# A hybrid encoder on one core: memory tokens turned by strips from row tile 4 on, one tile at a time, and later loads of natural tokens

## The chip, the core and the metric

The kernel runs on one core of one Trainium2 chip. The core has TensorE (PE: matmuls, with weight loads shown as PEld), VectorE (DVE), ScalarE (ACT), GpSimd (POOL) and SyncE (SP), and 16 DMA engines that move data between the chip's main memory and the core's on-chip memory. Engines run their own instructions in order and wait for each other by semaphores. The metric is the device time of one execution in microseconds; a kernel's time is the median of its runs.

## What is computed

Two layers of an encoder over 256 tokens of width 2048, all in float32. Each layer projects the normalised tokens, mixes them in three head groups, projects back and adds. The third group attends to 256 memory tokens, whose keys and values come from a projection that does not depend on x:

```python
for l in range(DEPTH):                                    # DEPTH = 2
    proj = rmsnorm(x, norm_g[l]) @ w_in[l]                # 2048 -> 7168, split in ten parts
    y_a = short_gated_conv(...) * silu(a_g)               # 768 columns
    y_d = rmsnorm(diff_attention(...), ...) * silu(d_g)   # 768 columns
    mkv = rmsnorm(mem, mem_norm_g[l]) @ w_mem_kv[l]       # mem: 256 x 2048 -> 512 keys, 512 values
    y_m = memory_attention(mq, mk, mv) * silu(m_g)        # 512 columns
    x = x + concat(y_a, y_d, y_m) @ w_out[l]
```

## The kernel before, in words

**Matrix products.** Every float32 operand is split into a high part (written by ACT) and a low part (the rest, written by DVE), and a product is three matmuls: high by high, high by low, low by high. Stationary operands are tokens with the contracted columns on the partitions, so tokens must be turned; moving operands are weights, 512 columns at a time. `split_T` (L257) writes both parts of one turned row tile (128 columns of all 256 tokens) into `memT` or `xT`.

**The memory stage** comes first: keys and values of both layers, before any work on x. It is one hand-written loop over 32 chunks g, sixteen row tiles k for each of two layers (L893 to L955). Chunk g multiplies row tile k of the memory tokens by 128 rows of `w_mem_kv[l]`, 1024 columns: half 0 is keys, half 1 values, two tiles of tokens, three matmuls each, so twelve matmuls. `operands(g)` (L812) prepares a chunk two chunks ahead: `token_parts` turns and splits the tokens (first layer alone), `w_parts` (L787) scales the weights by the norm's gain and splits them. `beside(g)` (L856) issues what stands beside the chunk: weights of chunk g + 4 (four raw buffers), loads and squares listed in the dictionaries `TOKENS`, `MEM_STRIPS`, `X_STRIPS`, `X_NATURAL`, `X_SQUARES`, and one small load of constants per chunk. `pin` keeps the program's order on an engine; what is not pinned is placed by the planner.

**Two ways of turning tokens.** Row tiles below `DEALT` (8) are loaded as natural tokens into `xs`, and TensorE turns them with an identity (`turned`, L795, two transposes per tile, into `pt`). Row tiles from `DEALT` on are loaded by strips: `strips_of` (L676) loads 512 columns of all tokens in four transfers of 128 KB, each to 32 partitions; DVE then turns blocks of 32 x 32 (`strips_turned`, L686), 128 x 1024 values in one instruction, which gives four row tiles at once. Their contracted columns are dealt over four tiles (column 4p + j to partition p of tile j), so the weights' rows are taken in the same order (`x_row_tiles`) and their gains from `gm_dealt` instead of `cva`. Natural tokens of all tiles are needed anyway for the sums of squares (`mem_squares`, ACT), from which `mem_stats` makes the row scales `stm`. x is turned by strips too (`x_turned`, L692), and its natural tokens are loaded into the same `xs` (`x_natural`) when the memory tokens there are done with; they are squared (`x_square`) and kept for the residual.

**Steps.** `run_side` (L231), at the end of each chunk, advances every generator in `tasks` that is due; `yield n` means n chunks until the next step. `later(g, n)` sets the first.

**The end of the stage.** When a layer's last row tile is done, `empty_keys` (L833) copies the key sums from PSUM (`kraw`, ACT) and `empty_values` (L839) the value sums, scaled by `stm`. Four accumulators exist; the first block of products over x (`block`, L293, called at L980) needs those that `kraw` frees. `keys_slowly` then normalises keys and turns them by transfers that POOL issues. `rest_of_constants` (L147) turns the small vectors into columns on TensorE.

**The rest** is twice: blocks over x in chunks of two row tiles (`load_w`, L280; ACT writes hi, DVE lo; PE L310 to L312), attention beside them, and the projection back.

Of the kernel before, what the change touches and what calls it, by code (L numbers as in the profile page):

```python
# [19 lines left out]
P = 128  # L20
D_MODEL = 2048
SEQ = 256
# [15 lines left out]
NA = P // B  # L38
PAIR_EVERY = 9
QT = NB // P  # L40
DEALT = 8


C_X, C_B, C_C, C_G = 0, 768, 1536, 2304
# [5 lines left out]
def encoder(ctx: ExitStack, tc: tile.TileContext, x, mem, norm_g, w_in, conv_w, conv_b,  # L50
# [21 lines left out]
    def nm(s):  # L72
        uid[0] += 1
        return f"{s}_{uid[0]}"
# [54 lines left out]
    def g_norm(l, k):  # L129
        return gx[:, l * KT + k:l * KT + k + 1]  # L130
# [83 lines left out]
    def later(g, n):  # L214
        due[id(g)] = chunk[0] + n
        return g
# [40 lines left out]
    def split_T(dst, k, src, gain, pin=False):  # L257

        hi, lo = dst[:, 0, k, :], dst[:, 1, k, :]
        if gain is None:  # L260
            both = (nc.scalar.copy(hi, src),
                    nc.vector.tensor_tensor(lo, src, hi.bitcast(F32), ALU.subtract))
        else:
            both = (nc.scalar.activation(hi, src, AF.Copy, scale=gain),
                    nc.vector.scalar_tensor_tensor(lo, src, gain, hi.bitcast(F32), ALU.mult, ALU.subtract))
        if pin:
            for i in both:
                tc.keep_in_program_order(i)
        made.add((id(dst), k))
# [403 lines left out]

    mem_done = set()

    def strips_of(src, at_once=1):  # L676

        st = tmp.tile([P, SEQ // B, B * QT], F32, tag="e", name=nm("xt"))
        for b in range(NA):
            pin(nc.sync.dma_start(  # L680
                st[b * B:(b + 1) * B], src[:, b * B * QT:(b + 1) * B * QT].rearrange("(n p) r -> p n r", p=B)))
            if (b + 1) % at_once == 0 and b + 1 < NA:
                yield
        return st

    def strips_turned(st):  # L686
        whole = tmp.tile([P, QT, SEQ], F32, tag="sh", name=nm("xf"))
        pin(nc.vector.transpose(whole.rearrange("p j (n i) -> p j n i", i=B),  # L688
                                st.rearrange("p n (c j) -> p j n c", j=QT)))
        return whole  # L690

    def x_turned(dst, l, q, src, at_once):  # L692


        st = yield from strips_of(src, at_once)
        yield 2
        whole = strips_turned(st)
        yield
        for j in range(QT):
            split_T(dst, q * QT + j, whole[:, j], g_norm(l, q * QT + j), pin=True)  # L700
            if j % 2:
                yield

    def x_next(dst, l, q):

# [25 lines left out]
    def mem_squares(c):  # L731

        for t in range(NT):
            sq = tmp.tile([P, NB], F32, tag="nat", name=nm("msq"), bufs=3)
            pin(nc.scalar.activation(sq, xs[:, t, c * NB:(c + 1) * NB], AF.Square, accum_out=ssm[:, t, c:c + 1]))
# [62 lines left out]
            pin(nc.tensor.transpose(pt[:, t * P:(t + 1) * P], xs[:, t, k * P:(k + 1) * P], ident))  # L798
        return pt

    dealt = {}

    def mem_turned(q, at_once):
        st = yield from strips_of(mem[:, q * NB:(q + 1) * NB], at_once)
        yield 2
        dealt[q] = strips_turned(st)

    def token_parts(g):
        if g < KT:
            split_T(memT, g, turned(g) if g < DEALT else dealt[g // QT][:, g % QT], None, pin=True)  # L810

    def operands(g):  # L812
        token_parts(g)
        w_parts(g)

    accs = {}

# [29 lines left out]
    def x_natural(c, t):  # L847
        pin(nc.sync.dma_start(xs[:, t, c * NB:(c + 1) * NB], x[t * P:(t + 1) * P, c * NB:(c + 1) * NB]))

    TOKENS = {0: 4, 1: 6, 8: 8, 9: 10, 10: 12, 11: 14}  # L850
    MEM_STRIPS = {2: 2, 4: 3}
    X_STRIPS = {12: 0, 16: 1, 20: 2, 24: 3}
    X_NATURAL = {14: (0, 0), 17: (0, 1), 20: (1, 0), 22: (1, 1), 24: (2, 0), 26: (2, 1), 28: (3, 0), 29: (3, 1)}
    X_SQUARES = {19: 0, 25: 1, 29: 2}

    def beside(g):  # L856


        if g + 4 < NG:
            if g in TOKENS:  # L860
                tokens(TOKENS[g], 2)
            weights(g + 4)
        if g in MEM_STRIPS:
            tasks.append(later(mem_turned(MEM_STRIPS[g], 2 if g == 2 else 1), 1))
        if g >= 2:
            for dst, src in islice(constants, 1):
                pin(nc.sync.dma_start(dst, src))
        if g in X_STRIPS:
            q = X_STRIPS[g]
            tasks.append(later(x_turned(xT, 0, q, x[:, q * NB:(q + 1) * NB], 1), 1))  # L870
        if g in (4, 8, 11, 13):
            mem_squares((4, 8, 11, 13).index(g))
        if g == 6:
            distance(1)
        if g == 13:
            tasks.append(later(mem_stats(), 1))
        if g == 21:
            tasks.append(later(rest_of_constants(), 1))
        if g in X_NATURAL:
            x_natural(*X_NATURAL[g])  # L880
        if g in X_SQUARES:
            for t in range(NT):
                x_square(X_SQUARES[g], t)

    row_sums = []

    def last_square():
        for t in range(NT):
            x_square(3, t)
        yield 2  # L890
        row_sums.append(stats_of(ssx, "st"))

    for _ in range(DEPTH):  # L893
# [7 lines left out]
    tokens(1, 1)  # L901
    weights(1, 0, NB)
    weights(1, NB, NB)
    tokens(2, 1)
    weights(2, 0, NB)
    weights(2, NB, NB)
    tokens(3, 1)
    weights(3)
    warm(6)
    distance(0)  # L910
    pv = ps_t.tile([P, NB], F32, tag="t", name="pva")
# [250 lines left out]
```

## Time and profile before

| | us |
|---|---|
| median of 3 runs (917.89 to 918.72) | 918.6 |
| the profiled execution | 918.26 |
| its span | 916.5 |
| PE busy in the span | 912.1 |
| DVE busy | 682.3 |
| ACT busy | 512.4 |
| first product of the memory stage | 5.04 |
| first product over x | 94.96 |

The granted TensorE clock is 1.000 over the span. Rows of the timeline read: start, duration (both us, from the span's start), engine, line, operation, output<-inputs, shape, count of merged instructions, and in brackets the idle time before it with what ended it. Rows of groups read: line, engine, operation, output<-inputs, shape, count | busy us, mean ns of one | idle us before them, and what ended it. Rows of windows read: stretch, its length, then busy us and count for PE, PEld, DVE, ACT and POOL, granted clock, DMA share, GB/s. SPq rows are issues of transfers by SP. 216 MB are moved in all, 236 GB/s over the span.

### The profile page before, as it was taken

Reading aid. Unit: us, or ns where it says so; the run is one execution under the profiler, and the core shown is the slowest. Engines: PE = TensorE matmul, PEld = TensorE weight load, DVE = VectorE, ACT = ScalarE, POOL = GpSimd, SP = SyncE. Lnnn points to the kernel's source line nnn. Section 1 sums busy time; section 2 is a strip of 40 time slices with the busy share of each in tenths; the row PEclk is TensorE's granted clock in tenths of the full one; section 3 lists DMA queues with packets and bytes.
Section 4 is the critical chain, followed back from the end, with each engine's and each line's share of the span. In section 5 each row is a group of like instructions: output and inputs, shape, how many; then the busy total and the mean of one; then the engine's idle time right before and its main releaser. Section 6 shows DMA issues by size and latency. Waiting matters only on the chain.

```text
span 916.5 us, 12329 instructions
## 1 busy us (share of the span) xinstructions
PE 912.1 (100%) x4167; PEld 758.0 (83%) x4167; DVE 682.3 (74%) x1216; ACT 512.4 (56%) x802; POOL 7.0 (1%) x18
## 2 busy tenths in 40 slices
PE   9999999999999999999999999999999999999998
PEld 7888888888888888888888888888888888888887
DVE  5888978857897787658677757878899786658553
ACT  6766745675554765545455544568555664446431
POOL 0001000000000000000000000000000000000000
PEclk9999999999999999999999999999999999999999
DMA  9999888876769989978687867886888979978662
GB/s 286 291 270 310 273 253 235 254 211 185 187 212 239 247 249 266 264 255 249 214 257 249 237 195 221 235 237 176 242 231 222 254 206 260 288 228 241 210 216 80
DMA packets 252964, 216.11 MB, mean 236 GB/s; under 512 B 131727, under 2 KB 180197, under 8 KB 252901
## 3 DMA queue, kind: packets, MB, share of 16 engines
q1 hardware_dynamic: 250740, 211.78, 80.5%
q0 software_dynamic: 672, 2.10, 0.6%
q10 hardware_dynamic: 1488, 1.46, 0.5%
q8 instruction: 32, 0.52, 0.2%
q14 instruction: 32, 0.25, 0.1%
HBM read 194.32 MB, written 20.97 MB: 235 GB/s over the span
## 4 chain that ended last, share of the span: by engine, by line
PE 91%; DMA 4%; DVE 2%; ACT 1%; issue 1%; SPq 0%; ACTq 0%; DVEq 0%
PE acc L311 29%; PE acc L310 29%; PE acc L312 29%; DMA raw<-in_w_mem_kv_dram 3%; PE po L480 1%; PE acc L827 1%; DMA raw<-in_w_in_dram 1%; DVE xf L688 1%; DVE lo L793 1%; ACT hi L792 1%; PE poT L469 1%; PE s L594 1%; PE s L593 1%; PE s L646 1%; DMA xt<-in_mem_dram 0%
## 5 line engine op out<-in xcount | busy, mean ns | idle before, releaser
L290 DVE TENSOR_TENSOR lo<-raw,hi 128x1024 fp32r<-128x1024 f32 x288 | 351.4, 1222 | 171.0 <-ACT hi L289 167.5
L289 ACT CAST hi<-raw 128x1024 fp32r<-128x1024 f32 x288 | 302.2, 1052 | 305.5 <-PE acc L312 235.9
L311 PE MATMUL acc<-lo,xT 128*128 128x512 f32 x896 | 349.2, 390 | 0.0
L312 PE MATMUL acc<-hi,xT 128*128 128x512 f32 x896 | 348.7, 389 | 0.0
L310 PE MATMUL acc<-hi,xT 128*128 128x512 f32 x896 | 347.7, 390 | 0.2 <-ACT kraw L836 0.2
L312 PEld LDWEIGHTS acc<-hi,xT 128*128 128x128 f32 x896 | 168.2, 188 | 34.7
L310 PEld LDWEIGHTS acc<-hi,xT 128*128 128x128 f32 x896 | 168.2, 188 | 34.7 <-ACT kraw L836 0.6
L311 PEld LDWEIGHTS acc<-lo,xT 128*128 128x128 f32 x896 | 168.3, 188 | 33.7
L312 PE MATMUL acc<-hi,yT 128*128 128x512 f32 (+1 forms) x258 | 100.0, 387 | 0.0
L310 PE MATMUL acc<-hi,yT 128*128 128x512 f32 (+1 forms) x258 | 100.0, 387 | 0.0
L311 PE MATMUL acc<-lo,yT 128*128 128x512 f32 (+1 forms) x258 | 99.9, 387 | 0.0
L827 PE MATMUL acc<-hi,memT 128*128 128x512 f32 (+1 forms) x260 | 70.5, 389 | 0.0
L310 PEld LDWEIGHTS acc<-hi,yT 128*128 128x128 f32 x258 | 48.4, 188 | 10.0
L311 PEld LDWEIGHTS acc<-lo,yT 128*128 128x128 f32 x258 | 48.4, 188 | 9.9
L312 PEld LDWEIGHTS acc<-hi,yT 128*128 128x128 f32 x258 | 48.4, 188 | 9.8
L827 PEld LDWEIGHTS acc<-hi,memT 128*128 128x128 f32 x260 | 47.9, 188 | 9.8 <-ACT hi L792 0.3
L827 PE MATMUL acc<-lo,memT 128*128 128x512 f32 (+1 forms) x130 | 39.7, 387 | 0.0
L827 PEld LDWEIGHTS acc<-lo,memT 128*128 128x128 f32 x130 | 24.3, 188 | 5.0
L793 DVE SCALAR_TENSOR_TENSOR lo<-raw,cva,hi 128x1024 fp32r<-128x1024 f32 (+2 forms) x21 | 21.4, 1026 | 6.5 <-ACT hi L792 5.4
L604 ACT ACTIVATE e<-e,mx 128x256 f32<-128x256 f32 x48 | 23.8, 498 | 1.4 <-DVE mx L600 1.3
L793 DVE SCALAR_TENSOR_TENSOR lo<-raw,gm_dealt,hi 128x1024 fp32r<-128x1024 f32 x16 | 20.5, 1279 | 4.6 <-ACT hi L792 4.5
L792 ACT ACTIVATE hi<-raw,cva 128x1024 fp32r<-128x1024 f32 (+2 forms) x21 | 19.7, 947 | 6.4 <-DMA raw<-in_w_mem_kv_dram 6.4
(162 smaller groups left out, 654.6 us busy)
## 6 DMA issues: line engine op xcount, KB each, us to landing
raw<-in_w_in_dram SPq DMA_DIRECT2D x192, 512.0 KB, 4.4
raw<-in_w_out_dram SPq DMA_DIRECT2D x64, 512.0 KB, 4.7
raw<-in_w_in_dram SPq DMA_DIRECT2D x64, 256.0 KB, 4.8
raw<-in_w_mem_kv_dram SPq DMA_DIRECT2D x29, 512.0 KB, 7.1
d<-sh SPq DMA_DIRECT2D x88, 128.0 KB, 3.9
sh<-d SPq DMA_DIRECT2D x72, 128.0 KB, 3.9
xt<-in_x_dram SPq DMA_DIRECT2D x16, 128.0 KB, 6.7
xs<-in_x_dram SPq DMA_DIRECT2D x8, 256.0 KB, 6.8
```

The costliest lines, as they stand in the source:

```text
L289: nc.scalar.copy(hi, raw)
L290: nc.vector.tensor_tensor(lo_, raw, hi.bitcast(F32), ALU.subtract)
L310: nc.tensor.matmul(acc[t], sh, hi, start=first, stop=False)
L311: nc.tensor.matmul(acc[t], sh, lo, start=False, stop=False)
L312: nc.tensor.matmul(acc[t], sl, hi, start=False, stop=last)
L469: nc.tensor.matmul(po, vp[:, v_part, k], e[:, e_part, k], start=k + v_part + e_part == 0, stop=k == NT - 1 and v_part == 1)
L480: nc.tensor.matmul(po[:, t, :], eT[:, i, t, k, :], v[:, k, h * P:(h + 1) * P], start=k == 0, stop=k == NT - 1)
L593: nc.tensor.matmul(s[c][:, i, :], qi, k_first(yT, c, h), start=True, stop=False)
L604: nc.scalar.activation(e[:, c, i], e[:, c, i], AF.Exp, bias=mx[:, c, i:i + 1], accum_out=sm[:, c, i:i + 1])
L792: pin(nc.scalar.activation(hi, raw, AF.Copy, scale=gain))
L793: pin(nc.vector.scalar_tensor_tensor(lo, raw, gain, hi.bitcast(F32), ALU.mult, ALU.subtract))
L827: pin(nc.tensor.matmul(accs[l, half][t][:, at:at + n], memT[:, token_part, k, t * P:(t + 1) * P], p, start=k == 0 and at == 0 and token_pa ...
```

## The change

- `DEALT` is 4: row tiles 4 to 7 of the memory tokens come by strips too, and are no longer turned on TensorE. This holds for weights and gains of both layers.
- Memory strips are turned one row tile at a time (`mem_turn`, 128 x 256 values), one tile ahead of its use, inside `operands`; x strips two row tiles at a time.
- Strips for tiles 4 to 7 are loaded ahead of the loop, with the first constant (`gm_dealt` of layer 0); tokens 2 and 3 come in one load. Weights of chunk 4 are split in two halves.
- Natural memory tokens 4 to 7 are loaded beside chunks 6 and 8 instead of 0 and 1; their squares, `mem_stats` and the other constants come later.
- Strips of x begin a chunk later, natural tokens of x two or more; those of the last 512 columns are loaded in the first block over x, where the last two pairs of squares are made.

```diff
-DEALT = 8
+DEALT = 4
...
-    def strips_turned(st):
-        whole = tmp.tile([P, QT, SEQ], F32, tag="sh", name=nm("xf"))
-        pin(nc.vector.transpose(whole.rearrange("p j (n i) -> p j n i", i=B),
-                                st.rearrange("p n (c j) -> p j n c", j=QT)))
-        return whole
+    def whole_tile():
+        return tmp.tile([P, QT, SEQ], F32, tag="sh", name=nm("xf"))
+
+    def turn_strips(whole, st, at, n):
+        pin(nc.vector.transpose(whole.rearrange("p j (n i) -> p j n i", i=B)[:, at:at + n],
+                                st.rearrange("p n (c j) -> p j n c", j=QT)[:, at:at + n]))
...
-        whole = strips_turned(st)
-        yield
-        for j in range(QT):
-            split_T(dst, q * QT + j, whole[:, j], g_norm(l, q * QT + j), pin=True)
-            if j % 2:
-                yield
+        whole = whole_tile()
+        for j in range(0, QT, 2):
+            turn_strips(whole, st, j, 2)
+            yield
+            for i in (j, j + 1):
+                split_T(dst, q * QT + i, whole[:, i], g_norm(l, q * QT + i), pin=True)
...
+    def mem_strips(q, at_once, apart=1):
+        strips_in[q] = yield from strips_of(mem[:, q * NB:(q + 1) * NB], at_once, apart)
+
+    def mem_turn(k):
+        q, j = divmod(k, QT)
+        if j == 0:
+            dealt[q] = whole_tile()
+        turn_strips(dealt[q], strips_in[q], j, 1)
...
     def operands(g):
+        if g == DEALT:
+            mem_turn(g)
         token_parts(g)
-        w_parts(g)
+        if DEALT <= g < KT - 1:
+            mem_turn(g + 1)
+        if g == DEALT:
+            w_parts(g, 0, NB)
+            w_parts(g, NB, NB)
+        else:
+            w_parts(g)
...
-    TOKENS = {0: 4, 1: 6, 8: 8, 9: 10, 10: 12, 11: 14}
-    MEM_STRIPS = {2: 2, 4: 3}
-    X_STRIPS = {12: 0, 16: 1, 20: 2, 24: 3}
-    X_NATURAL = {14: (0, 0), 17: (0, 1), 20: (1, 0), 22: (1, 1), 24: (2, 0), 26: (2, 1), 28: (3, 0), 29: (3, 1)}
-    X_SQUARES = {19: 0, 25: 1, 29: 2}
+    TOKENS = {6: 4, 8: 6, 9: 8, 10: 10, 11: 12, 12: 14}
+    MEM_SQUARES = {4: 0, 11: 1, 13: 2, 14: 3}
+    MEM_STRIPS = {2: 2, 5: 3}
+    X_STRIPS = {13: 0, 17: 1, 21: 2, 25: 3}
+    X_NATURAL = {16: (0, 0), 19: (0, 1), 22: (1, 0), 25: (1, 1), 28: (2, 0), 30: (2, 1)}
+    X_SQUARES = {23: 0, 27: 1}
...
-        if g >= 2:
+        if g >= 10:
             for dst, src in islice(constants, 1):
                 pin(nc.sync.dma_start(dst, src))
...
-        if g in (4, 8, 11, 13):
-            mem_squares((4, 8, 11, 13).index(g))
+        if g in MEM_SQUARES:
+            mem_squares(MEM_SQUARES[g])
...
-        if g == 13:
+        if g == 14:
             tasks.append(later(mem_stats(), 1))
-        if g == 21:
+        if g == 28:
             tasks.append(later(rest_of_constants(), 1))
...
-    def last_square():
+    def last_squares():
+        for t in range(NT):
+            x_natural(3, t)
+            yield
+        for t in range(NT):
+            x_square(2, t)
+        yield 2
         for t in range(NT):
             x_square(3, t)
-        yield 2
+        yield
         row_sums.append(stats_of(ssx, "st"))
...
-    tokens(2, 1)
+    tokens(2, 2)
     weights(2, 0, NB)
     weights(2, NB, NB)
-    tokens(3, 1)
     weights(3)
+    for _ in mem_strips(1, NA):
+        pass
+    for dst, src in islice(constants, 1):
+        pin(nc.sync.dma_start(dst, src))
...
-    tasks.append(later(last_square(), 2))
+    tasks.append(later(last_squares(), 1))
```

More of the change, by code (lines that the diff above doesn't have):

```diff
@@ L674, in encoder, with strips_of @@
     mem_done = set()
-    def strips_of(src, at_once=1):
+    def strips_of(src, at_once=1, apart=1):
         st = tmp.tile([P, SEQ // B, B * QT], F32, tag="e", name=nm("xt"))
@@ L682, in strips_of @@
             if (b + 1) % at_once == 0 and b + 1 < NA:
-                yield
+                yield apart
         return st
-    def strips_turned(st):
-        whole = tmp.tile([P, QT, SEQ], F32, tag="sh", name=nm("xf"))
-        pin(nc.vector.transpose(whole.rearrange("p j (n i) -> p j n i", i=B),
-                                st.rearrange("p n (c j) -> p j n c", j=QT)))
-        return whole
+    def whole_tile():
[3 more added lines that the diff above has]
+                                st.rearrange("p n (c j) -> p j n c", j=QT)[:, at:at + n]))
     def x_turned(dst, l, q, src, at_once):
@@ L696, in x_turned @@
         yield 2
-        whole = strips_turned(st)
-        yield
-        for j in range(QT):
-            split_T(dst, q * QT + j, whole[:, j], g_norm(l, q * QT + j), pin=True)
-            if j % 2:
-                yield
+        whole = whole_tile()
[4 more added lines that the diff above has]
+                split_T(dst, q * QT + i, whole[:, i], g_norm(l, q * QT + i), pin=True)
     def x_next(dst, l, q):
@@ L799, in turned @@
         return pt
-    dealt = {}
-    def mem_turned(q, at_once):
-        st = yield from strips_of(mem[:, q * NB:(q + 1) * NB], at_once)
-        yield 2
-        dealt[q] = strips_turned(st)
+    dealt, strips_in = {}, {}
+    def mem_strips(q, at_once, apart=1):
[5 more added lines that the diff above has]
+        turn_strips(dealt[q], strips_in[q], j, 1)
     def token_parts(g):
@@ L863, in beside @@
         if g in MEM_STRIPS:
-            tasks.append(later(mem_turned(MEM_STRIPS[g], 2 if g == 2 else 1), 1))
-        if g >= 2:
+            tasks.append(later(mem_strips(MEM_STRIPS[g], 2, 1 if g == 2 else 2), 1))
+        if g >= 10:
             for dst, src in islice(constants, 1):
@@ L885, in encoder @@
     row_sums = []
-    def last_square():
+    def last_squares():
[5 more added lines that the diff above has]
+        yield 2
         for t in range(NT):
             x_square(3, t)
-        yield 2
+        yield
         row_sums.append(stats_of(ssx, "st"))
```

## The prediction

> **What bounds the kernel now.** I read the page first (span, engines, chain), then what TensorE waited for in the memory stage, then TensorE's own timeline.
>
> ```profile
> span 916.5 us, 12329 instructions
> PE 912.1 (100%) x4167; PEld 758.0 (83%) x4167; DVE 682.3 (74%) x1216; ACT 512.4 (56%) x802; POOL 7.0 (1%) x18
> PE 91%; DMA 4%; DVE 2%; ACT 1%; issue 1%; SPq 0%; ACTq 0%; DVEq 0%
> ...
> PE warm L125 <- PEq L1148: 0.8, 1, 0.8
> PE acc L310 <- ACT kraw L836: 0.2, 1, 0.2
> ```
>
> PE is busy for 912.1 of 916.5 us and holds 91% of the chain that ended last. The last two rows are all that PE waited for in the first 140 us (total, times, longest): the start, and one wait of 0.2 us. "Busy" has modelled ends, so starts tell more:
>
> ```profile
> 14.28 0.62 PE L827 MATMUL acc<-hi,memT 128*128 128x512 f32 x2
> 14.74 0.60 PE L798 MATMUL pt<-ident,xs 128*128 128x128 f32 x4
> 17.50 0.62 PE L827 MATMUL acc<-hi,memT 128*128 128x512 f32 x2
> 20.49 0.62 PE L827 MATMUL acc<-hi,memT 128*128 128x512 f32 x2
> 23.48 1.07 PE L827 MATMUL acc<-hi,memT 128*128 128x512 f32 x4
> 26.20 1.07 PE L827 MATMUL acc<-hi,memT 128*128 128x512 f32 x4
> 94.17 0.61 PE L827 MATMUL acc<-lo,memT 128*128 128x512 f32 x2
> 94.96 0.50 PE L310 MATMUL acc<-hi,xT 128*128 128x512 f32 x1 [0.17 <-ACT kraw L836]
> 95.30 0.39 PE L311 MATMUL acc<-lo,xT 128*128 128x512 f32 x1
> 95.53 0.39 PE L312 MATMUL acc<-hi,xT 128*128 128x512 f32 x1
> ```
>
> The matmul rows at 14.28, 17.50, 20.49, 23.48 and 26.20 are the first products of chunks 3 to 7. Chunk 6 (from 23.48 to 26.20) has twelve products and no transposes: 2.72 us, 0.227 each. So the stage runs at the pace of its matmuls, and a load that comes earlier buys nothing by itself. What can be gained is instructions taken off PE and the small holes. The hole at the end: the two products from 94.17 should be followed at 94.17 + 2 x 0.227 = 94.62, the first one of the block over x starts at 94.96 (0.34 lost), and the next 0.34 later instead of 0.23 (0.11 more): 0.45 in all.
>
> **Transposes removed (DEALT 8 to 4).** Row tiles 4 to 7 no longer pass through PE: eight transposes go, a pair per tile. Tiles 4 and 5 were turned inside chunk 3, tile 6 in chunk 4, tile 7 in chunk 5. Chunk 3 took 17.50 - 14.28 = 3.22, chunks 4 and 5 took 2.99 each; above 2.72 that is 0.50 + 0.27 + 0.27 = **-1.04 us**, on the path.
>
> **What takes their place: a chain through DVE and ACT.** Tile 4 must now be turned on DVE, copied by ACT, and the weights split, all between the end of chunk 3's operands and the first product of chunk 4.
>
> ```profile
> L688 DVE STREAM_TRANSPOSE xf<-xt 128x1024 f32<-128x1024 f32 x6 | 12.1, 2014 | 0.0
> L793 DVE SCALAR_TENSOR_TENSOR lo<-raw,gm_dealt,hi 128x1024 fp32r<-128x1024 f32 x16 | 20.5, 1279 | 4.6 <-ACT hi L792 4.5
> L793 DVE SCALAR_TENSOR_TENSOR lo<-raw,cva,hi 128x512 fp32r<-128x512 f32 x7 | 5.2, 750 | 1.3 <-ACT hi L792 1.3
> L792 ACT ACTIVATE hi<-raw,gm_dealt 128x1024 fp32r<-128x1024 f32 x16 | 18.3, 1147 | 2.6 <-DMA raw<-in_w_mem_kv_dram 2.6
> L792 ACT ACTIVATE hi<-raw,cva 128x512 fp32r<-128x512 f32 x7 | 5.0, 724 | 0.9 <-DMA raw<-in_w_mem_kv_dram 0.9
> L261 ACT CAST memT<-xf 128x256 fp32r<-128x256 f32 x8 | 3.2, 394 | 6.5 <-DVE xf L688 6.5
> L262 DVE TENSOR_TENSOR memT<-xf,memT 128x256 fp32r<-128x256 f32 x8 | 3.4, 422 | 1.1 <-ACT memT L261 0.9
> ...
> 14.57 0.75 DVE L793 SCALAR_TENSOR_TENSOR lo<-raw,cva,hi 128x512 fp32r<-128x512 f32 x1 [0.20 <-ACT hi L792]
> ```
>
> A single turn is a quarter of 2014 ns: 0.50 at least. Halving a weight split took 750 instead of 1279, so 2 x 750 - 1279 = 221 ns of it do not scale; with that a quarter turn is 0.22 + 1.79/4 = 0.67. I take 0.60, between the two, because DVE instructions overlap a little back to back. DVE is done with chunk 3 at 14.57 + 0.75 = 15.32, unchanged. From there, with 0.05 for a hand-over: turn 4 ends 15.92; ACT's copy 16.37, its weight half 17.09; DVE's low part of tile 4 ends 16.8, turn 5 17.4, low weights (first half) 18.15, second half 18.9, low part of tile 5 19.3, turn 6 19.9, low weights of chunk 5 21.2. PE without the transposes wants chunk 4 at 14.28 + 2.72 = 17.00 and gets it at 17.14 (0.14); wants the low half four products later at 18.05 and gets it at 18.2 (0.15); wants chunk 5's low weights at 20.01 + 0.91 = 20.92 and gets them at 21.25 (0.33). Sum **+0.62 us** (0.3 with turns of 0.50, 0.8 with 0.67). From chunk 6 on DVE needs 0.42 + 0.60 + 1.28 = 2.30 per chunk against PE's 2.72, so nothing accumulates. Splitting chunk 4's weights in two costs ACT 2 x 724 - 1147 = 0.3 and DVE 0.22, both counted; without the split the first product would wait 0.4 longer.
>
> [...]
>
> **Strips first, natural tokens later (SP and DMA).** Ahead of chunk 4's weights SP now issues four strip loads of 128 KB and the constant gm_dealt, instead of one 256 KB load of tokens; tokens 2 and 3 come in one load, and the loads for tiles 4 to 7 drop out until chunks 6 and 8.
>
> ```profile
> 0.00:4.00 4.00, 3.21 (x9) 1.23 (x10) 0.19 (x1) 1.70 (x2) 1.37 (x8) 1.00 0.45 132
> 4.00:8.00 4.00, 4.00 (x24) 3.15 (x23) 2.92 (x6) 2.79 (x6) 0.00 (x0) 1.00 0.98 318
> 8.00:12.00 4.00, 4.00 (x20) 3.19 (x20) 2.90 (x6) 2.74 (x5) 0.00 (x0) 1.00 1.05 391
> 12.00:16.00 4.00, 4.00 (x22) 3.29 (x21) 2.59 (x5) 1.99 (x5) 0.00 (x0) 1.00 1.05 375
> 16.00:20.00 4.00, 4.00 (x20) 3.24 (x19) 3.33 (x5) 3.52 (x6) 0.00 (x0) 1.00 1.09 246
> ...
> 9.37 3.31 SPq L785 DMA_DIRECT2D raw<-in_w_mem_kv_dram  x2
> 12.73 0.43 SPq L867 DMA_DIRECT2D gm_dealt<-in_mem_norm_g_dram  x1
> ```
>
> The last column is GB/s. In MB, 0.53 have moved by 4 us and 1.80 by 8. Weights 0 to 3 and tokens 0 to 3 are 2.62 MB, so they are in at about 10.1. Strips (0.52) and weights 4 (0.52) follow: at 375 GB/s by 12.9, at the 246 of the window in which strips were loaded before by 14.3; about 1 us more for landing. ACT wants those weights at 16.4 and DVE the strips at 15.3 (in by 13.2 even at the slow rate). Weights 5 follow 1.4 to 2.1 later, 15.3 to 17.4, wanted at 18.2. Cost 0, hidden behind operands of chunk 3; the cover is about 1 us. Weights 5 and 6 (the row at 9.37) wait on SP for free buffers as before; that wait, 3.31 for two issues, also covers the constants, 0.43 of SP each, which now stand ahead of chunk 4 (one) and in chunks 10 to 24 (the rest). In the stage 0.5 MB of strips come in and 0.5 MB of x (columns 3) go out into the first block.
>
> **Squares, statistics and constants moved.** Squares of the last tokens and mem_stats come a chunk later; they must be done before the values are emptied:
>
> ```profile
> 44.21 1.14 ACT L792 ACTIVATE hi<-raw,cva 128x1024 fp32r<-128x1024 f32 x1
> 50.99 1.27 ACT L842 ACTIVATE mv<-acc,stm 128x512 f32<-128x512 f32 x2
> 53.40 0.84 PE L827 MATMUL acc<-hi,memT 128*128 128x512 f32 x3
> ...
> L735 ACT ACTIVATE msq<-xs 128x512 f32<-128x512 f32 x8 | 4.9, 617 | 0.0
> L189 DVE TENSOR_TENSOR rsa<-rsa,ssum 128x2 f32<-128x2 f32 x3 | 0.5, 158 | 0.1
> L724 ACT ACTIVATE sq<-xs 128x512 f32<-128x512 f32 x6 | 3.8, 627 | 4.2 <-DMA xs<-in_x_dram 4.1
> ```
>
> The squares now follow the row at 44.21, end at about 47, and the fifteen small DVE steps end by about 50.9, so mv still starts at 51 and ends at 52.3, while PE (0.4 earlier by then) wants the space at 53.0. Cost 0, at worst 1 us. Constants of layer 0 go from chunk 21 to chunk 28: one PE transpose moves, its price stays, and a dozen small DVE steps fall among the last chunks. In the last row ACT stood 4.1 us before squares of x, waiting for natural tokens that now have four chunks or more to land; PE did not feel it, so its end gains nothing. POOL's key transfers stand before and after as they did. Two loads and four squares in the first block lie beside 43 us of matmuls; nothing waits for their sums until its end.
>
> **The end of the stage.**
>
> ```profile
> 92.35 0.90 ACT L264 ACTIVATE xT<-xf,gx 128x256 fp32r<-128x256 f32 x2
> 93.38 1.05 ACT L289 CAST hi<-raw 128x1024 fp32r<-128x1024 f32 x1
> 94.33 1.07 ACT L836 COPY kraw<-acc 128x512 f32<-128x512 f32 x2
> ```
>
> The copy kraw, for which PE waits at 94.96, stands on ACT behind 0.90 us of x parts and a weight cast. The last strips of x are turned a chunk later, in halves, so those parts fall behind kraw, and 0.5 MB less is loaded ahead of the first weights of x. I take 0.34 of the 0.45: **-0.34 us**. Ends: -0.45, or +1.05 if the order on ACT puts another cast ahead of kraw.
>
> **Sum.** -1.04 + 0.62 - 0.34 = -0.76. The profiled execution took 918.26 us (span 916.5 and 1.8 around it), 0.34 under the median of 918.6 and within the runs' 917.89 to 918.72. So 917.5 against its own time, **917.8** against the median.
>
> **Rivals.** (1) PE gains more. If a transpose held PE for its whole duration, eight would give 2.35 instead of 1.04:
>
> ```profile
> L798 PE MATMUL pt<-ident,xs 128*128 128x128 f32 x16 | 3.2, 294 | 0.0
> ```
>
> Then 918.6 - 2.35 + 0.62 - 0.34 = 916.5. The starts speak against it: four cost 0.50. [...] (2) It does not do what it says: waits take the place of the transposes. With turns of 0.67, the values a microsecond late, and kraw no earlier: -1.04 + 0.8 + 1.0 = +0.8, 919.4; for it speaks the cover of only 1 us in two places. (3) Slower: transfers of strips to 32 partitions hold the queue down. From 10.1 us at 200 GB/s (5.0 us per MB), weights 4 would land at 16.3, 5 at 19, 6 (with 0.26 MB of strips) at 22.9 and 7 at 26.8; low parts come 0.5, 1.5 and 2 later than wanted, some 4 us, minus 1.4: about 921.2. It decides from a rate under about 215 GB/s between 10 and 27 us; the lowest full row above is 246, so it is unlikely.
>
> **How the numbers follow.** What a measurement here can tell from no change is about 0.2%, 1.84 us: 916.76 to 920.44. Forecast (917.1 to 918.4) 0.61; rival 1 0.05; rival 2 (918.4 to 920.4) 0.24; rival 3 0.10. Rival 1 and the forecast's lower edge make faster 0.07; rival 3 and rival 2's upper edge slower 0.11; the rest, 0.82, is the same. The range goes from 916.9 (all gains without stall, -1.49, and the runs' scatter) to 919.6 (rival 2).
>
> **What would show it.** Right: pt only x8; chunks 3 to 5 with no 2.99; first product of chunk 6 near 23.1; PE holes of tenths before chunks 4 and 5 with DVE lo or ACT hi as releaser; the first product of x near 94.2 without kraw ahead. Wrong: a PE wait of over 1 us on a memory weight or strip load, or mv later than 52.

## The result, and the profile after

The changed kernel takes 926.35 us (median of 6 runs, 921.52 to 927.67) against 918.55 (6 runs) for the kernel before: 1.0077 times as long, with a 95% interval of 1.0054 to 1.0099. The forecast was 917.8, at most 919.6. The profiled execution took 927.67, 9.4 more than that of before, and its span is 9.4 longer.

First the page (span, engines, chain), then what TensorE waited for in the first 140 us (total, times, longest):

```profile
span 925.9 us, 12337 instructions
PE 916.1 (99%) x4159; PEld 756.0 (82%) x4159; DVE 683.9 (74%) x1235; ACT 512.3 (55%) x803; POOL 7.0 (1%) x18
PE 88%; DMA 8%; DVE 1%; ACT 1%; issue 1%; SPq 0%; ACTq 0%; DVEq 0%
```

```profile
PE acc L840 <- ACT hi L793: 2.0, 4, 0.6
PE acc L840 <- DVE lo L794: 1.7, 2, 1.0
...
PE acc L840 <- ACT kraw L849: 0.6, 1, 0.6
```

Eight of TensorE's instructions are gone (4167 to 4159), as the change says. But transfers hold 8% of the chain where they held 4%, and in the memory stage (products at L840, weight splits at L793 and L794, turns at L690) TensorE now waits for both halves of the split. Its timeline shows where:

```profile
14.80 1.09 PE L840 MATMUL acc<-hi,memT 128*128 128x512 f32 x4
18.23 1.20 PE L840 MATMUL acc<-hi,memT 128*128 128x512 f32 x4 [0.50 <-ACT hi L793]
21.09 1.07 PE L840 MATMUL acc<-hi,memT 128*128 128x512 f32 x4
23.84 1.07 PE L840 MATMUL acc<-hi,memT 128*128 128x512 f32 x4
26.56 1.07 PE L840 MATMUL acc<-hi,memT 128*128 128x512 f32 x4
28.38 0.73 PE L840 MATMUL acc<-lo,memT 128*128 128x512 f32 x2 [0.76 <-DVE lo L794]
30.81 1.20 PE L840 MATMUL acc<-hi,memT 128*128 128x512 f32 x4 [0.30 <-ACT hi L793]
37.58 1.20 PE L840 MATMUL acc<-hi,memT 128*128 128x512 f32 x4 [0.62 <-ACT hi L793]
40.85 1.07 PE L840 MATMUL acc<-hi,memT 128*128 128x512 f32 x4
102.78 0.61 PE L840 MATMUL acc<-lo,memT 128*128 128x512 f32 x2
103.55 0.50 PE L310 MATMUL acc<-hi,xT 128*128 128x512 f32 x1 [0.15 <-ACT kraw L849]
103.89 0.40 PE L311 MATMUL acc<-lo,xT 128*128 128x512 f32 x1
```

The rows at 14.80, 18.23, 21.09, 23.84 and 26.56 are the first products of chunks 3 to 7; they stand 0.4 to 0.7 us behind those of before, and the distance doesn't grow. From chunk 7 (26.56) to chunk 11 (40.85) it takes 14.29 instead of 4 x 2.72 = 10.88: 3.4 us are lost there. The first product over x comes at 103.55, 8.6 after that of before, so another 4.8 is lost between chunk 11 and the end of the stage (a table at the end of the experiments shows where), and 0.8 more behind it. (A hole is longer than its bracket: TensorE's weight loads stood idle 1.18, 0.74 and 1.04 us ahead of the rows at 28.38, 30.81 and 37.58, whose brackets say 0.76, 0.30 and 0.62.)

ACT's wait for raw weights in the first 100 us (total, times, longest), before:

```profile
ACT hi L792 <- DMA raw<-in_w_mem_kv_dram: 8.9, 12, 1.5
```

and after:

```profile
ACT hi L793 <- DMA raw<-in_w_mem_kv_dram: 19.3, 17, 3.0
```

The single turns of after in the same stretch:

```profile
L690 DVE STREAM_TRANSPOSE xf<-xt 128x256 f32<-128x256 f32 x12 | 7.6, 636 | 2.6 <-DMA xt<-in_mem_dram 2.5
```

ACT stood 19.3 us before raw weights where it had stood 8.9, and DVE 2.5 before strips where it had stood none. The engines are hardly busier (DVE 683.9 us against 682.3, ACT 512.3 against 512.4); transfers land later. Issue to landing, median, of weights (512 KB) and of memory strips (128 KB) issued between 8 and 45 us, in the kernel before:

```profile
raw<-in_w_mem_kv_dram SPq DMA_DIRECT2D x15, 512.0 KB, 5.6
xt<-in_mem_dram SPq DMA_DIRECT2D x8, 128.0 KB, 4.7
```

and after:

```profile
raw<-in_w_mem_kv_dram SPq DMA_DIRECT2D x13, 512.0 KB, 8.0
xt<-in_mem_dram SPq DMA_DIRECT2D x10, 128.0 KB, 8.8
```

These medians rest on few loads, since the trace ties only some landings to their issue: 8 of the 15 weights and 4 of the 8 strips before, 3 of 13 and 2 of 10 after. The waits below do not depend on that.

DVE's timeline shows a strip landing late. In the kernel before, the turn of tiles 8 to 11 stood behind the low part of weights 7 and found its strips there:

```profile
24.02 2.00 DVE L688 STREAM_TRANSPOSE xf<-xt 128x1024 f32<-128x1024 f32 x1
```

In after, the turn at 26.53 is that of tile 8; it is done with the operands of chunk 7 and stands on DVE ahead of the low part of weights 7, for which TensorE waits at 28.38:

```profile
26.53 0.63 DVE L690 STREAM_TRANSPOSE xf<-xt 128x256 f32<-128x256 f32 x1 [2.14 <-DMA xt<-in_mem_dram]
27.09 1.24 DVE L794 SCALAR_TENSOR_TENSOR lo<-raw,gm_dealt,hi 128x1024 fp32r<-128x1024 f32 x1
```

And the chain of waits that ended last between 20 and 45 us (start, duration, what) shows how it goes on: a load of weights (those of chunk 8, issued at 19.66), its split, and then the load that a freed buffer lets go.

```profile
19.66 9.84 DMA raw<-in_w_mem_kv_dram
...
29.61 1.16 ACT hi L793
...
32.96 1.17 DVE lo L794
...
34.16 8.71 DMA raw<-in_w_mem_kv_dram
```

### The profile page after: what moved, and what is told of

The parts are those of the page before. It is cut to its first block, busy times and chain, and to the rows that moved or that the text cites. A ratio compares the mean times of both kernels' runs of the same rounds, so it can differ in the third digit from the quotient of the medians.

```text
span 925.9 us, 12337 instructions
## 1 busy us (share of the span) xinstructions
PE 916.1 (99%) x4159; PEld 756.0 (82%) x4159; DVE 683.9 (74%) x1235; ACT 512.3 (55%) x803; POOL 7.0 (1%) x18
## 4 chain that ended last, share of the span: by engine, by line
PE 88%; DMA 8%; DVE 1%; ACT 1%; issue 1%; SPq 0%; ACTq 0%; DVEq 0%
PE acc L310 28%; PE acc L312 28%; PE acc L311 28%; DMA raw<-in_w_mem_kv_dram 4%; DMA xs<-in_x_dram 1%; PE po L480 1%; DMA raw<-in_w_in_dram 1%; DMA xt<-in_mem_dram 1%; DVE lo L794 1%; PE poT L469 1%; PE s L594 1%; PE s L593 1%; PE s L646 1%; DMA xs<-in_mem_dram 0%; ACT hi L793 0%
## 5 line engine op out<-in xcount | busy, mean ns | idle before, releaser
L840 PE MATMUL acc<-hi,memT 128*128 128x512 f32 (+1 forms) x260 | 71.6, 394 | 2.8 <-ACT hi L793 2.0
L840 PEld LDWEIGHTS acc<-hi,memT 128*128 128x128 f32 x260 | 47.5, 188 | 16.3 <-ACT hi L793 4.3
L840 PE MATMUL acc<-lo,memT 128*128 128x512 f32 (+1 forms) x130 | 40.5, 393 | 2.1 <-DVE lo L794 1.7
L794 DVE SCALAR_TENSOR_TENSOR lo<-raw,gm_dealt,hi 128x1024 fp32r<-128x1024 f32 (+1 forms) x25 | 30.7, 1230 | 8.1 <-ACT hi L793 7.5
L793 ACT ACTIVATE hi<-raw,gm_dealt 128x1024 fp32r<-128x1024 f32 (+1 forms) x25 | 27.5, 1112 | 12.8 <-DMA raw<-in_w_mem_kv_dram 12.4
L840 PEld LDWEIGHTS acc<-lo,memT 128*128 128x128 f32 x130 | 23.7, 188 | 9.6 <-DVE lo L794 5.0
L690 DVE STREAM_TRANSPOSE xf<-xt 128x512 f32<-128x512 f32 (+1 forms) x28 | 25.2, 898 | 2.6 <-DMA xt<-in_mem_dram 2.5
```

The costliest lines, as they stand in the source:

```text
L793: pin(nc.scalar.activation(hi, raw, AF.Copy, scale=gain))
L794: pin(nc.vector.scalar_tensor_tensor(lo, raw, gain, hi.bitcast(F32), ALU.mult, ALU.subtract))
L840: pin(nc.tensor.matmul(accs[l, half][t][:, at:at + n], memT[:, token_part, k, t * P:(t + 1) * P], p, start=k == 0 and at == 0 and token_pa ...
```

## The experiments

The expectations give their theories letters; A to D are explained where they first stand. Three more came up in turn. E: the stage is bound by what the transfers move, because strips that land on 32 partitions move slowly (in one run, h1, E is the bytes alone). F: a loop; a late operand frees its raw buffer late, the weights four chunks on are issued late and land late. G: two outlets together, the raw buffers and the turn of tile 8. Times stand beside runs of the kernel before on the same chip, and ratios have 95% intervals.

**Which part of the change.** e1 keeps tiles 4 to 7 natural, with all the rest of the change:

```diff
-DEALT = 4
+DEALT = 8
-    TOKENS = {6: 4, 8: 6, 9: 8, 10: 10, 11: 12, 12: 14}
+    TOKENS = {0: 4, 1: 6, 9: 8, 10: 10, 11: 12, 12: 14}
-    for _ in mem_strips(1, NA):
-        pass
```

> The changed kernel with one part undone: row tiles 4 to 7 come as natural tokens again (loaded beside chunks 0 and 1, turned on TensorE), with no strip loads ahead of the loop. All the rest of the change stays: single turns of tiles 8 to 15, x in halves, later constants, squares and loads of x. Theory A (the early strip loads and what hangs on them slow the transfers, and weights land late): 918 to 920. Theory B (the later squares, constants and loads of x stall ScalarE and with it TensorE): still 923 or more. Theory C (the chain of single turns through VectorE and ScalarE): in between, 920 to 922, since eight of twelve single turns stay.

Measured: 918.62, ratio 1.0001 (0.9991 to 1.001). e2 keeps strips for tiles 4 to 7 and puts everything on x, its squares and the constants back (also `X_NATURAL`, `last_square` and the whole turn of x):

```diff
-    X_STRIPS = {13: 0, 17: 1, 21: 2, 25: 3}
+    X_STRIPS = {12: 0, 16: 1, 20: 2, 24: 3}
-    X_SQUARES = {23: 0, 27: 1}
+    X_SQUARES = {19: 0, 25: 1, 29: 2}
-        if g >= 10:
+        if g >= 2:
...
-        if g == 28:
+        if g == 21:
```

> The changed kernel with the other part undone: strips of x, natural tokens of x, squares of x, the two last columns' loads, the small constants (one per chunk from chunk 2) and their turning stand as in the kernel before, and x is turned whole. Row tiles 4 to 7 by early strips and single turns stay. Theory A: as slow as the changed kernel, 923 to 927. Theory B: near 918.5. Theory C: 922 to 926.

Measured: 926.41, 1.009 (1.0068 to 1.0112). So the strips for tiles 4 to 7, and what hangs on them, cost the time. The later constants, squares and loads of x, and the single turns of tiles 8 to 15, cost nothing by themselves.

**How strips land.** In e3 and e4 (after and before) a strip load goes to all 128 partitions in two pieces each instead of 32 in eight; bytes, pieces and places in the program stay, the tokens come in another order.

```diff
-                st[b * B:(b + 1) * B], src[:, b * B * QT:(b + 1) * B * QT].rearrange("(n p) r -> p n r", p=B)))
+                st[:, b * NT:(b + 1) * NT], src[:, b * B * QT:(b + 1) * B * QT].rearrange("(n p) r -> p n r", p=P)))
```

> The changed kernel, in which each strip load keeps its bytes, its source and its pieces of 512 bytes, but lands on all 128 partitions (two pieces each) instead of on 32 (eight pieces each); the turned tokens are then other tokens, so this kernel leaves the right order of tokens out. Theory D (landing on 32 partitions is what slows strip loads and the weights beside them): GB/s between 8 and 36 us goes up from about 280 to 350 or more, and the time falls to 917 to 919. If it is the number or the place of the pieces in memory: unchanged, 922 to 927.

> The kernel before with the same change of where strips land (tokens in another order, as in the run with the changed kernel). It had no stall for transfers on TensorE, so all theories expect 918 to 918.6; theory D also expects GB/s between 48 and 80 us to go up from 275 or the DMA share to fall below 1.0.

Measured: e3 918.07, 0.9991 (0.9982 to 1.0001); e4 918.15, 0.9998 (0.9988 to 1.0007). The whole loss is gone in e3, with all dependences of the change in place, and wide strips alone change nothing in e4. So the narrow landing is a cause without which there is no loss. Landing times in e3:

```profile
raw<-in_w_mem_kv_dram SPq DMA_DIRECT2D x15, 512.0 KB, 5.7
xt<-in_mem_dram SPq DMA_DIRECT2D x9, 128.0 KB, 5.2
```

They are near those of before (they, too, rest on few landings, 4 and 2). The turn of tile 8 waits for nothing, and TensorE has no wait after the start:

```profile
23.43 0.65 DVE L690 STREAM_TRANSPOSE xf<-xt 128x256 f32<-128x256 f32 x1
```

The windows (8 to 36 us; share of the DMA engines' time, then GB/s) of after and of e3 show the rate (before, it was 309 GB/s):

```profile
8.00:36.00 28.00, 26.32 (x113) 19.98 (x112) 19.53 (x31) 15.25 (x27) 0.00 (x0) 1.00 1.08 270
```

```profile
8.00:36.00 28.00, 27.96 (x124) 22.35 (x123) 22.08 (x35) 17.63 (x31) 0.00 (x0) 1.00 0.95 312
```

The rate rose from 270 to 312, not to the 350 that was expected, while the time fell as expected. In e4 the rate from 48 to 80 us rose from 275 to 288, as theory D had it.

**What the extra traffic costs if nobody waits for it.** f1 and f2 add to the kernel before, behind weights 3, four unread strip loads of 128 KB, to 32 and to 128 partitions; h2 adds the narrow ones to e1, which then moves the bytes of after.

```diff
     weights(3)
+    for b in range(NA):
+        pin(nc.sync.dma_start(dummy[b * B:(b + 1) * B], mem[:, NB + b * B * QT:NB + (b + 1) * B * QT]...))
```

> The kernel before, with four more strip loads (512 KB, each to 32 partitions, into a tile that nobody reads) at the place where the change puts its own, after the weights of chunk 3. No transposes, turns, weights or constants are changed. Theory D (loads that land on 32 partitions hold up all transfers): narrow bytes go from 3.1 to 3.7 MB; in the kernel before, the windows from 48 to 80 us moved 8.8 MB, of which 1.7 MB were strips; with the rest at 390 GB/s the strips went at about 124 GB/s, so 0.5 MB more cost 4.2 us of transfers. The stage had a few us of cover in all, so 920 to 926, with weights late on ScalarE as in the changed kernel. Theory C (the chain of turns is what costs): 918.4, no change.

> The same four extra loads with the same bytes, source and 512-byte pieces, landing on 128 partitions. Theory D: 0.5 MB at the full rate is 1.4 us of transfers, hidden: 918 to 919.5. If it is the bytes or the count of pieces or the places in the queue that cost: as slow as with the narrow loads.

> The kernel with tokens 4 to 7 natural (918.6) with four more narrow strip loads of 512 KB in all, into a tile nobody reads, at the place where the changed kernel has its own. Bytes and narrow bytes of the stage are then those of the changed kernel (926.4), but TensorE turns tiles 4 to 7 and nothing waits for these strips. Theories D and E (bytes and narrow landings): 923 to 927. Theory F (what waits for the strips matters): 919 to 921.5, like the four extra narrow loads in the kernel before (921.0).

Measured: f1 921.03, 1.0032 (1.0016 to 1.0049); f2 919.68, 1.0015 (1.0002 to 1.0027); h2 919.36, 1.0013 (1.0004 to 1.0023). f2 lies 0.2 above what theory D expected. Traffic alone costs 1 to 3 us, and f1 and f2 do not tell narrow from wide, since their intervals overlap. h2 carries the narrow loads of after, and its weights and strips land nearly as late (medians of 7.2 and 8.5 us of what the trace ties). It loses 1.1 us against before, a seventh of the 7.8 that after loses. So the landing alone isn't the cause either; it must meet operands that wait for it.

**Other queue, first strips, fewer bytes.** g1 issues every second strip load from POOL; g2 makes only the four loads for tiles 4 to 7 wide; h1 is g2 without natural tokens 4 to 7 (0.5 MB less; their squares are taken of other tokens).

```diff
-            pin(nc.sync.dma_start(
+            pin((nc.gpsimd if b % 2 else nc.sync).dma_start(
```

```diff
+            to, p = (st[:, b * NT:(b + 1) * NT], P) if wide else (st[b * B:(b + 1) * B], B)
...
-        strips_in[q] = yield from strips_of(mem[:, q * NB:(q + 1) * NB], at_once, apart)
+        strips_in[q] = yield from strips_of(mem[:, q * NB:(q + 1) * NB], at_once, apart, q == 1)
...
-    TOKENS = {6: 4, 8: 6, 9: 8, 10: 10, 11: 12, 12: 14}
+    TOKENS = {9: 8, 10: 10, 11: 12, 12: 14}   # h1
```

> The changed kernel, every result as in the reference; every second strip load (blocks 1 and 3) is issued by POOL instead of SP, so that loads to two groups of 32 partitions can be under way at once. Theory D with transfers of one queue served in order: two groups at once double the rate of the strips, most of the stalls go, 918 to 921. If loads of a group don't run beside each other, or POOL's issue is slow: 924 to 930.

> The changed kernel; only the four early strip loads (tiles 4 to 7) land on 128 partitions, the other 24 stay on 32 (tiles 4 to 7 then hold other tokens, so the right order of these is left out). Theory D: narrow bytes are 3.1 MB as in the kernel before, so 918 to 919.5. If the slow transfers come from the later strips, which the change also moves: 921 to 926.

> The changed kernel with the four early strip loads landing on 128 partitions (922.2 as it stood), now also without the natural tokens 4 to 7 (two loads of 256 KB beside chunks 6 and 8; their squares are taken of other tokens, so the row scales of the memory tokens are left out). Bytes and narrow bytes of the stage are then those of the kernel with tokens 4 to 7 natural (918.6), and what differs is how tiles 4 to 7 are turned. Theory E (the stage has room for about 28 MB at this mix, and 0.5 MB above it is what costs): 918.5 to 919.5. Theory F (the chain of single turns leaves operands just in time, so raw buffers are freed late and the weights four chunks on are issued late): 921 to 923.

Measured: g1 924.9, 1.0072 (1.0057 to 1.0087); g2 922.23, 1.0048 (1.0031 to 1.0064); h1 922.25, 1.0042 (1.0027 to 1.0057). g1 and g2 fell into the second case of their expectations, h1 where F put it. In g1 the strips overtook the first weights (POOL was busy for 3.43 us of the first 4, in after for 1.37), so chunk 3 began 3.0 us later than before (after: 0.5); chunks 7 to 11 then lost nothing, and the first product over x came 4.1 late instead of 8.6. Behind it g1's profile loses 2.3 more, which was not followed up. Half of the loss hangs on the first four loads; half a megabyte less changes nothing, so bytes alone are out. In both g2 and h1 the turn of tile 8 still waits for narrow strips (1.21 and 2.10). In g2 that wait cost TensorE next to nothing (chunks 7 to 11 took 11.03 instead of 10.88); most of what g2 and h1 lose goes at the end of the stage (table below).

**A narrow load by itself.** i1 and i2 put the four unread loads at the very head of the kernel before, ahead of the first tokens, narrow and wide, one run each.

```diff
+    for b in range(NA):
+        pin(nc.sync.dma_start(dummy..., mem...))
     pin(nc.scalar.dma_start(va, ...))
```

> The kernel before with the four narrow strip loads (512 KB, to 32 partitions each, into a tile nobody reads) ahead of every other load on SP, where nothing else is under way but ACT's three loads: the price of the loads by themselves. Theory D at 124 GB/s: first product and span later by about 4.2 us, 922 to 923.

> The same four loads at the head, landing on 128 partitions. Theory D at 390 GB/s: later by about 1.4 us (the four issues of 0.45 us on SP are 1.8), 920. If pieces of 512 bytes are what is slow: as with the narrow ones.

Measured: 924.33 and 923.29, more than the 922 to 923 and the 920 that were expected; the last section shows why. The tokens that stand behind them come at 8.04 in i1:

```profile
8.04 0.69 PE L798 MATMUL pt<-ident,xs 128*128 128x128 f32 x2 [4.34 <-DMA xs<-in_mem_dram]
```

and at 6.36 in i2:

```profile
6.36 0.69 PE L798 MATMUL pt<-ident,xs 128*128 128x128 f32 x2 [2.61 <-DMA xs<-in_mem_dram]
```

So 512 KB landing on 32 partitions at a time hold what follows back by 8.04 - 6.36 = 1.7 us more than the same pieces on 128, in one run of each. The four loads themselves took 3.4 us from issue to landing in i1 and 2.6 in i2 (medians of what the trace ties), and from 4 to 6 us 267 GB/s moved in i1 and 336 in i2. Rival 3 of the prediction goes the same way.

**The loop over raw buffers.** j1 adds a fifth raw buffer to after (j2 to before), so weights g + 5 go out when weights g are split. j3 turns tile g + 1 behind the low weights of chunk g; j4 does both.

```diff
-            raws[g] = wp.tile(..., bufs=4)
+            raws[g] = keep.tile(..., tag="mqT") if g % 5 == 4 else wp.tile(..., bufs=4)
-            weights(g + 4)
+            weights(g + 5)
...
+    weights(4)
```

```diff
-        if DEALT <= g < KT - 1:
-            mem_turn(g + 1)
         if g == DEALT:
...
+        if DEALT <= g < KT - 1:
+            mem_turn(g + 1)
```

> The kernel after with a fifth buffer for raw weights of the memory stage (every fifth chunk's raw weights go to a tile that is free until the first layer), so weights of chunk g + 5 are issued when chunk g's are split, and weights 4 stand at the head behind the strips. Theory F (the loss is a loop: a late operand frees its raw buffer late, the weights four chunks on are issued late, and the way from issue to the low part is longer than the 10.88 us that four chunks give): with five buffers the way may take 13.6 us, most of the 7.5 us comes back: 918.5 to 920.5, no first product of chunks 11 to 28 more than 2 us later than before. Theory E (the stage is bound by what the transfers move at the rate that strips to 32 partitions leave): an earlier issue only queues up earlier, 924 to 927.

> The control: the kernel before with the same fifth raw buffer. It has no wait on weights in the stage but the start, so both theories expect no change, 918 to 919; if it is faster or slower by over 1 us, j1 has to be read against it.

> The kernel after, with the turn of tile g + 1 behind the low part of the weights of chunk g on DVE instead of ahead of it. Theory F: raw buffers come free some 0.63 us earlier in chunks 4 to 14, and a late strip no longer holds up the split of weights that have landed; the loss shrinks by 1.5 to 4 us, 922 to 925. Theory E: 926 to 927, since the transfers are the same. If the turns are late next and hold ACT's copies, it is slower, 927 to 929.

> Both edits, fifth raw buffer and later turn. Theory F: at most what the fifth buffer alone gives, 917.5 to 919.5, and if all stalls are gone the removed transposes show: 917.5. Theory E: 924 to 927.

Measured: j1 925.32, 1.0078 (1.0065 to 1.0091); j2 918.43, 1.0 (0.9991 to 1.0009); j3 928.11, 1.0106 (1.009 to 1.0121); j4 930.71, 1.0131 (1.0117 to 1.0145). F as the whole cause falls: j1 lies where E expected it, and j4 outside what either expected. j2 shows that the buffer by itself changes nothing. In j1 ACT's wait for raw weights fell as F said, from 19.3 us to 4.7 in the first 100, but the wait moved. The wait, DVE and TensorE in j1:

```profile
ACT hi L794 <- DMA raw<-in_w_mem_kv_dram: 4.7, 6, 1.5
```

```profile
30.64 0.63 DVE L690 STREAM_TRANSPOSE xf<-xt 128x256 f32<-128x256 f32 x1 [4.75 <-DMA xt<-in_mem_dram]
```

```profile
32.49 1.15 PE L841 MATMUL acc<-lo,memT 128*128 128x512 f32 x2 [3.14 <-DVE lo L795]
```

More weights in flight, later strips: tile 8's turn waits 4.75 instead of 2.14. j3 says nothing on F, because my edit built a loop of its own (the case that the last sentence of the expectation allows for): turn, ACT's copy, high weights, low weights, next turn, each waiting for the last. DVE's rows come back every 39.55 - 36.19 = 3.36 us, more than the 2.72 of a chunk:

```profile
36.19 0.62 DVE L690 STREAM_TRANSPOSE xf<-xt 128x256 f32<-128x256 f32 x1
...
39.55 0.62 DVE L690 STREAM_TRANSPOSE xf<-xt 128x256 f32<-128x256 f32 x1
```

**Both outlets.** k1 turns tile 8 with its own chunk; k2 has the fifth buffer as well.

```diff
-        if g == DEALT:
+        if g in (DEALT, 8):
             mem_turn(g)
         token_parts(g)
-        if DEALT <= g < KT - 1:
+        if DEALT <= g < KT - 1 and g != 7:
             mem_turn(g + 1)
```

> The kernel after, with one instruction moved: tile 8 is turned with its own chunk's operands and no longer with those of chunk 7, where the turn stands ahead of the low part of weights 7 on DVE and waits 2.14 us for strips that land late. Theory G (two outlets: weights that wait for raw buffers, and the turn of tile 8 that wants late strips a chunk early): the hole of 0.9 before the low half of chunk 7 goes, the late weights 8 and 10 stay; 923.5 to 925.5. If the waiting turn is the whole cause: 918 to 920. If it is nothing: 926 to 927.

> Both outlets closed: tile 8 turned with its own chunk, and the fifth raw buffer. Transfers are those of after, narrow strips and all. Theory G: the 3.1 us hole before chunk 8 of the kernel with five buffers goes, and the weights land in time; 918.5 to 921. Theory E (the transfers bring too little by chunk 12 whatever waits for them): a hole moves to the next turn or weights, 923 to 927.

Measured: k1 924.02, 1.0062 (1.0042 to 1.0082); k2 925.28 (922.82 to 928.15), 1.0076 (1.0054 to 1.0097). k1's time is where G put it, but its profiled execution (927.37, the longest of the six) does not show G's way there: the turn of tile 8 no longer waits, and the low weights of chunk 7 are late all the same, now because their raw weights are (ACT's longest wait for raw weights is 3.3 us):

```profile
27.02 1.28 DVE L794 SCALAR_TENSOR_TENSOR lo<-raw,gm_dealt,hi 128x1024 fp32r<-128x1024 f32 x1 [3.02 <-ACT hi L793]
28.22 0.63 DVE L690 STREAM_TRANSPOSE xf<-xt 128x256 f32<-128x256 f32 x1
```

k2's time is not where G put it: 918.5 to 921 was expected, and it lies where E did. Its profiled execution (span 922.0) shows where it loses. TensorE's first products of chunks 0, 4 and 25:

```profile
7.28 1.15 PE L841 MATMUL acc<-hi,memT 128*128 128x256 f32 x6 [1.94 <-ACT hi L794]
...
20.86 1.16 PE L841 MATMUL acc<-hi,memT 128*128 128x512 f32 x4
...
78.24 1.07 PE L841 MATMUL acc<-hi,memT 128*128 128x512 f32 x4
```

From chunk 4 to chunk 25 it takes 57.38, as the 57.66 of e3 (17.48 to 75.14), and the holes of chunks 7 to 11 are gone. This is with the narrow loads of after, at no better a rate than after's (247 in the same window):

```profile
20.00:36.00 16.00, 16.00 (x71) 12.89 (x70) 14.72 (x22) 12.31 (x22) 0.00 (x0) 1.00 1.09 250
```

What k2 loses lies elsewhere: the first product came at 7.28 instead of 5.04 because the first weights were late (ACT waited 2.9 us in all for raw weights, 2.8 of it at once), and from chunk 25 to the first product over x it took 22.14 instead of 19.37, 2.8 more than before, with ACT waiting 10.6 in all for natural tokens of x ahead of their squares. In that one execution, then, the middle of the stage runs through with both outlets closed; what landings its trace ties to their issue are also shorter than after's (issued in the first 45 us, 6.5 us for weights and 6.7 for strips, against 8.0 and 8.3). That the two outlets explain the median is not shown.

**Where each run loses.** The stretches between TensorE's first products, in the one profiled execution of each run (us):

| | chunk 7 to 11 | 11 to 26 | 26 to the first over x |
|---|---|---|---|
| before | 10.88 | 41.23 | 16.65 |
| after | 14.29 | 43.75 | 18.95 |
| e1 (natural) | 10.88 | 40.80 | 17.48 |
| e2 (x as before) | 13.19 | 43.35 | 19.65 |
| e3 (wide) | 10.88 | 41.06 | 16.75 |
| h2 (natural, extra narrow) | 10.88 | 41.35 | 16.75 |
| g1 (two queues) | 10.88 | 43.08 | 16.75 |
| g2 (first four wide) | 11.03 | 42.25 | 19.68 |
| h1 (as g2, fewer bytes) | 12.54 | 40.80 | 20.34 |
| j1 (fifth buffer) | 15.91 | 40.80 | 19.82 |
| k1 (tile 8 with its chunk) | 14.63 | 41.39 | 20.48 |
| k2 (both) | 10.88 | 40.80 | 19.42 |

(The turning of small constants, 0.43, lies in the second stretch of before and e2 and in the third of the others.) So there is a third place, which neither F nor G names: in the last stretch after, e2, g2, h1, j1, k1 and k2 lose 2 to 3.5 us, j4 1.2, g1 and j3 nothing. In after ACT stands there before a square of x, which in its order is ahead of a split of weights:

```profile
88.24 0.63 ACT L725 ACTIVATE sq<-xs 128x512 f32<-128x512 f32 x1 [2.90 <-DMA xs<-in_x_dram]
```

Such waits make 7.4 us in the first 100 of after and 10.6 in k2, but 7.4 in e1 too, which loses only 0.4 there. No run moves these squares alone, so this is a reading and not a test.

## Why the prediction was wrong, point by point

- **The step that failed** is "Strips first, natural tokens later", costed "0, hidden behind operands of chunk 3; the cover is about 1 us". That step had the strips at the head landed by 13.2 and weights 4 by 15.3 even at its slow rate. The 1 us in it for landing was an estimate; in before half 0 of weights 2 bears it out: the 1.72 MB issued up to it had moved by 7.8 us (221 GB/s), if loads move in the order of their issue, and ACT's wait for it ended at 8.80. Measured in after, the turn of tile 4 got its strips at 16.21, after a wait of 0.36, and ACT got weights 4 at 17.46; chunk 4 began 0.73 late. Two things were left out. Tile 8 is now turned on DVE ahead of the low weights of chunk 7 (before, behind them), and the last two of its strips, issued from 16.26 on, are there only at 26.5; before, issued from 16.22 on, they were there by 24.02. And lateness isn't paid once, against the prediction's "so nothing accumulates": a raw buffer freed late sends the weights four chunks on late, and these, too, take longer to land (8.0 us against 5.6). Measured: 3.4 us between chunks 7 and 11, 8.6 by the first product over x, 9.4 in all in the profiled execution and 7.8 in the medians, where the step said nothing. That the narrow landing is behind it is shown by e3, and that it costs only where operands wait for it by h2; which wait costs how much stays open.
- **Rival 3** named the place and the direction, strips to 32 partitions, at a chance of 0.10. Its price (921.2) and its bound (a rate under about 215 GB/s between 10 and 27 us) were wrong. That stretch in after ran at 270:

```profile
10.00:27.00 17.00, 16.50 (x73) 12.86 (x72) 11.62 (x19) 10.77 (x19) 0.00 (x0) 1.00 1.10 270
```

  The loss came at a rate that the bound called safe, and k2 ran its middle without those holes at 250. My reading, from k2's one profile, is that what counts is when a strip lands behind what is queued, and what stands behind it in order.
- **Transposes removed, -1.04, and the chain through DVE and ACT, +0.62.** After hides both, so I read them from e3:

```profile
14.75 1.08 PE L840 MATMUL acc<-hi,memT 128*128 128x512 f32 x4
17.48 1.18 PE L840 MATMUL acc<-hi,memT 128*128 128x512 f32 x4
20.44 1.08 PE L840 MATMUL acc<-hi,memT 128*128 128x512 f32 x4
23.20 1.07 PE L840 MATMUL acc<-hi,memT 128*128 128x512 f32 x4
```

  Chunks 3 to 5 take 8.45 there, against 9.20 before: -0.75. The floor is 3 x 2.72 = 8.16, so if the transposes' 1.04 came off in full, the chain costs 0.29, half of the 0.62. A single turn takes 0.636, a little more than the 0.60 taken. The overlap that the 0.60 was chosen for is there: in after the weights behind the turn at 26.53 start at 27.09, 0.07 before it ends.
- **Squares, statistics and constants, "cost 0, at worst 1 us".** In e3 the values cost 0.26 (chunks 16 to 18). Chunks 25 to 31 took 0.43 more than before and chunks 18 to 25 0.43 less, which is the price of the constants moving as forecast. So with wide strips the term is near its low end. In after it is not: chunks 15 to 17 lost 1.65 (ACT had waited 1.70 for raw weights ahead of `kraw`, and `mv` came at 57.61). One reading was wrong from the start: natural tokens of x do not all "have four chunks or more to land". The last before the squares of chunk 27 are loaded beside chunk 25, and ACT waited 2.90 for them (the row at 88.24).
- **The end of the stage, -0.34.** In after it didn't come: 102.78 + 2 x 0.227 = 103.24 against 103.55, and then 0.34, so 0.42 of the old 0.45 is still there; two casts of late x weights went ahead of `kraw`. In e3, from the first product of chunk 31 to the first over x, it came to -0.33.
- **The sum.** With strips landing wide, the first product over x stands 0.35 ahead of before, of the 0.76 forecast, with e3's chunk 3 0.5 late; behind it e3's profile loses 0.7 again, which is not explained. Its median, 918.07, is 0.3 under the 918.36 of before on the same chip, and the interval reaches no change. So in e3 the terms but the transfer step held within some tenths inside the stage; that the change would then be worth its 0.76 is not shown.

What stays open: how after's loss divides between raw buffers, the turn of tile 8 and the squares of x (k2, with the first two closed, still loses 6.8), whether E, which j1 and k2 fit and h2 does not (919.36 where it expected 923 to 927), holds a part of it, and why after's start was late. No version ran that beats before beyond its interval; e3 is the nearest and turns another order of tokens.

## What to carry to other kernels

A load that is hidden when nobody waits for it early isn't hidden when operands are made to wait for it: cost a moved load by its landing time under the traffic around it, at each place where it is wanted, not by mean GB/s and one deadline. Look at what stands in order behind the waiting instruction; a turn done one tile ahead on DVE held the weights of the chunk before. And when one wait is taken away, see in the profile whether it has only moved, as from weights to strips in j1.

## What the runs showed of the hardware

- Strips of 512-byte pieces that land on 32 partitions cost more than the same pieces on 128: 1.7 us per 512 KB at an otherwise quiet head (i1, i2), and 8.8 against 5.2 us from issue to landing in the loaded stage (after, e3; medians of two landings each). Other loads slow with them: weights 8.0 against 5.7 (of three and four).
- A hole can cost more than its length. Chunk 0, from its first product to that of chunk 1, took 3.26 us before (5.04 to 8.30), 5.20 in i1 (9.44 to 14.64) after 4.34 without work, 5.27 in i2 (7.76 to 13.03) after 2.61, and 4.86 in k2 (7.28 to 12.14) after 1.94. In i1 the granted clock was 1.00 from 4 to 6 us, 0.73 from 6 to 8 and 0.50 from 8 to 12, the stretch after the hole; in k2 it was 1.00 from 4 to 8 and 0.57 from 8 to 12, behind the shortest of the three holes. For i2 the windows print 1.00 up to 14, yet the six products from 7.76 took 1.84, as long as those of i1 (1.84 from 9.44) and not the 1.09 of before. After how long without work the clock drops is not shown. Windows of i1, then of k2, and the products of i2:

```profile
8.00:12.00 4.00, 3.96 (x16) 3.26 (x17) 2.96 (x6) 1.81 (x3) 0.00 (x0) 0.50 0.95 314
```

```profile
8.00:12.00 4.00, 4.00 (x18) 3.46 (x17) 1.99 (x4) 2.11 (x5) 0.00 (x0) 0.57 0.94 265
```

```profile
7.76 1.84 PE L827 MATMUL acc<-hi,memT 128*128 128x256 f32 x6
```
